# A hybrid diffusion block on one NeuronCore: scores and value products from split operands, fewer PE runs for decay and modulation, last mixer outputs kept in SBUF

## The chip, the core and the metric

The kernel runs on one core of a Trainium2 chip. The time is device time in microseconds (us) from launch to end of one execution. In this text PE is the tensor engine (matrix products), DVE the vector engine, ACT the scalar engine, POOL the GpSimd engine; SP issues most DMAs and ACT's queue issues some. SBUF is the working memory, PSUM the eight banks (128 partitions x 512 fp32) that PE writes.

## The reference, cut to what matters

Two layers over 256 latent tokens, 256 context tokens and 2,048 channels, all in fp32. Layer 0 has 16 attention heads and 32 SSD (Mamba-2) heads on one input projection; layer 1 is a gated short convolution.

```python
# layer 0: neighbourhood attention heads and bidirectional Mamba-2 heads side by side
q = rms_norm(heads(cols(p, COL_Q, ...)), q_norm_g);  k = rms_norm(...);  v = heads(...)
...
s_lat = jnp.einsum('bqhd,bkhd->bhqk', qr, kb) * scale + bias          # scores, lattice
s_ctx = jnp.einsum('bqhd,bkhd->bhqk', qr, k_ctx) * scale              # scores, context
pr = softmax(concatenate([s_lat, s_ctx]))
ya = einsum('bhqk,bkhd->bqhd', pr_lat, vb) + einsum('bhqk,bkhd->bqhd', pr_ctx, v_ctx)
...
w = cb[..., None] * decay * dtc[:, None]                              # SSD chunk of 128
y = jnp.einsum('bijgr,bjgrp->bigrp', w, xc)                           # decay product
...
out = jnp.concatenate([ya * silu(gate), yb], axis=-1) @ w_out         # 32 outputs of 128 channels
x = x + gate[:, None] * out
# every layer: shift, scale, gate = split(silu(c) @ ada_w + ada_b, 3)   (the modulation)
# layer 1: h @ w_in (4 parts), gated short convolution, @ w_out
```

The four latent rows and the 256 context tokens make 512 keys, so a head's scores are 256 queries by 512 keys, and its value product is 256 queries by 512 keys by 128 channels.

## The kernel before, in words

**Number format of the projections.** A large product a x w is made from split operands: a high half in the type fp32r (a copy of the fp32 number into that type) and a low half, the difference. Three products, high x high, low x high and high x low, go into the same bank. The weights come by DMA into `raw` buffers, ACT makes the high half `wH` (L401), DVE the low half `wL` (L408). Everything small is plain fp32 on PE: the scores (`KT` by `QT`, L1000), the value products (`Vt` by `P`, L1050), the transposes (L192), the decay products and the modulation sums. PE runs one plain fp32 product as two instructions, so the profile counts 64 for the 32 score products.

**The order is written by a planner.** Program order on each engine is made in Python at build time. The projections are the backbone: `proj` walks over K blocks and emits the backbone's products; after every few products `pump` looks at side tasks (Python generators such as `kq_gen`, `head_gen`, `group_gen`, `gemv_gen`, `mix_gen`), and lets one go on where `may` finds that the class `Plan` (a running estimate of every engine's clock and of each buffer's readiness) has its operands ready: a PE step of an attention or SSD task is placed only when they are ready 700 ns ahead of PE. Tasks hold shares of the pools: `NTMP` = 10 buffers of 128x512 (`tmp`), 9 of 128x256 (`half`), the 8 banks. `banks(n)` forces tasks on until n banks are free.

**Where the changed parts stand.** Attention runs in four groups of four heads. `kq_gen` normalises, transposes on PE, and writes K with an ACT copy into `KT` (L954) and Q with a DVE multiplication by the norm weight into `QT` (L956). `head_gen` makes two score products of 512 columns (L1000), adds the bias and takes the maximum on DVE (L1005), takes the exponential on ACT (L1010), scales on DVE (L1015), transposes on PE, copies to `PT` with ACT (L1042; two buffers, used by the heads in turn), and makes four value products of 256 columns (L1050), which DVE multiplies by the gate (L1054). `group_gen` makes, for each of 8 SSD groups, two times (b = 0, 1) four decay products of 64 output rows and 128 columns (`xtm` by `tmp`, L1358), in two separate runs; two of 64 rows stand side by side in the array. `gemv_gen` sums the modulation rows: DVE accumulates `acc` over the weights (L795), then four PE products with a matrix of ones and 32 output rows add up the partitions; there are 16 such sums. `put_mix` (L911) sends each of 32 mixer outputs (128 x 256) to DRAM, and `mix_gen` (L1478) reads them back in pairs, and ACT and DVE split them (L1488, L1489) into the buffers of the layer's input, once that input is no longer needed (`free_rows`). The output projection then reads them.

Of the kernel before, what the change touches and what calls it, by code (L numbers as in the profile page):

```python
# [31 lines left out]
for _name, _w in (("ident", 128), ("sel", 2), ("mhalf", 32), ("strip", 640), ("mask", 64)):  # L32
    _coff[_name] = (_n, _n + _w)
    _n += _w
# [107 lines left out]
def kernel(ctx: ExitStack, tc, x, cx, ada_w, ada_b, w_in, w_out, sc_in, sc_out, rpb, small, const,  # L142
# [19 lines left out]
    NTMP, NHALF, NRAW, NW = 10, 9, 5, 3  # L162
# [7 lines left out]
    KT, QT, Vt, gt = st([128, 4, 512], "KT"), st([128, 4, 256], "QT"), st([128, 4, 512], "Vt"), st([128, 4, 256], "gt")  # L170
# [68 lines left out]
    def may(task, hor, isurg):  # L239
# [17 lines left out]
        if eng == "PE":  # L257
            return rdy + (0 if isurg else 800) <= now + 100
# [71 lines left out]
    def give(pool, *bs):  # L330
        pool.extend(bs)
# [12 lines left out]
    U, ONES, L = strip[:, 128:256], strip[:, 256:384], strip[:, 384:512]  # L344
# [432 lines left out]
    acc = st([128, 512], "acc")  # L777
    n_back = [0]

    def gemv_gen():  # L780
        for n in range(16):
            lay = 0 if n < 4 else 1
            c0 = 4096 + n * 512 if n < 4 else (n - 4) * 512
            yield W_("DVE", nb=0)
            E(V.memset(acc, 0.0))
            E(DMA.dma_start(acc[:1, :], ada_b[lay:lay + 1, c0:c0 + 512]))
            for k in range(8):
                yield when(lambda: not (("gem", n, k) not in RAW))
                yield W_("DVE", RAW["gem", n, k][1], acc)
                raw, v = RAW.pop(("gem", n, k))  # L790
                ngem[0] -= 1
                for j in range(2):
                    if j:
                        yield W_("DVE", acc)
                    E(V.scalar_tensor_tensor(out=acc, in0=v[:, j], scalar=csil[:, 2 * k + j:2 * k + j + 1], in1=acc,  # L795
                                             op0=ALU.mult, op1=ALU.add))
                give_raw(raw)
                issue()
            yield W_("PE", acc, nb=1)
# [20 lines left out]
    rowb = mrb = st([128, 128], "rowb")  # L820
# [101 lines left out]
    def kq_gen(key, a, ps, nt, stat, dst, banked):  # L922
# [23 lines left out]
        for t in range(nt):  # L946
# [34 lines left out]
    b0 = rpbs[0, :, :]  # L981
    s4s = [st([128, 8], f"s4_{k}") for k in range(4)]

    def head_gen(a, h):
        hd = 4 * a + h
        bt, s4, P = bias[hd % 2], s4s[hd % 4], PT[hd % 2]
# [39 lines left out]
        yield W_("PE", KT[:, h, :], QT[:, h, :], nb=1)  # L1026
# [10 lines left out]
        scale_(1)  # L1037
        for qt in range(2):
            yield W_("PE", sps[qt], nb=1)
            pt = trans(qt)  # L1040
            yield W_("ACT", pt)
            E(S.copy(P[:, :, qt * 128:(qt + 1) * 128], four(pt)))  # L1042
# [4 lines left out]
        yield W_("PE", P, Vt, nb=1)  # L1047
# [803 lines left out]
```

## Time and profile before

| what | value |
|---|---|
| median of 3 runs (lowest to highest) | 1819.94 us (1819.16 to 1823.07) |
| profiled execution, its own time | 1820.47 us |
| its span, first to last instruction | 1818.7 us |
| granted PE clock, mean | 0.998 |
| ACT busy, share of span | 775.2 us, 43% |
| DMA moved | 376.90 MB, 207 GB/s |

A group row of the profile reads: line, engine, operation, out<-in, shapes, xcount, then busy us, mean ns of one, and the engine's idle time before them with what ended it. Matrix products are pipelined: a row's duration includes the latency, so a PE product's cost is read from the start of one to the start of the next, in the timeline. A timeline row has the start and the duration in us; equal neighbours are merged into one row.

### The profile page before, as it was taken

What the parts mean: (1) busy time and instruction counts of PE and PEld (TensorE: products, weight loads), DVE (VectorE), ACT (ScalarE), POOL (GpSimd) and SP (SyncE); (2) the same over time, 40 slices, a digit from 0 to 9 for tenths busy, and PEclk for the clock granted to TensorE, in tenths of its full rate; (3) what the DMA queues carried; (4) which work ended last, traced back from release to release, by engine and by line L of the source; (5) the groups of instructions that cost most, each with busy time, mean ns of one, the idle gap of its engine ahead of it and who ended that gap; (6) DMA issues with size and microseconds to landing.
All of it is one profiled execution on the core that took longest, in us unless ns stands there. A gap on an engine that the chain in (4) does not pass through costs nothing. (4 is left out here: it accounts for less than half of the span.)

```text
span 1818.7 us, 26323 instructions
## 1 busy us (share of the span) xinstructions
PE 1784.1 (98%) x9961; PEld 1488.1 (82%) x9961; DVE 1259.5 (69%) x2041; ACT 775.2 (43%) x1364; POOL 32.4 (2%) x28
## 2 busy tenths in 40 slices
PE   5999999999999999999999999999999999999998
PEld 4677988878888878888877898788878888888887
DVE  5566775887575877575877686776667776565665
ACT  5422543455232455232454343544445444444442
POOL 0000100001000001000001000000000000000000
PEclk9999999999999999999999999999999999999999
DMA  9987644576655576755576566678867786666664
GB/s 327 339 293 247 214 144 134 171 212 203 216 165 166 169 210 203 218 163 172 167 205 196 163 182 186 195 232 282 270 228 226 232 261 188 187 188 188 187 208 152
DMA packets 249216, 376.90 MB, mean 207 GB/s; under 512 B 32656, under 2 KB 104048, under 8 KB 249088
## 3 DMA queue, kind: packets, MB, share of 16 engines
q1 hardware_dynamic: 239792, 366.64, 65.5%
q10 hardware_dynamic: 9296, 8.57, 1.5%
q8 instruction: 78, 1.28, 0.3%
q14 instruction: 50, 0.41, 0.1%
HBM read 368.70 MB, written 7.77 MB: 207 GB/s over the span
## 5 line engine op out<-in xcount | busy, mean ns | idle before, releaser
L401 ACT CAST wH<-raw 128x1024 fp32r<-128x1024 f32 (+1 forms) x439 | 457.7, 1043 | 710.2 <-PE bank L188 556.2
L408 DVE TENSOR_TENSOR wL<-raw,wH 128x1024 fp32r<-128x1024 f32 (+1 forms) x439 | 532.0, 1214 | 283.8 <-ACT wH L401 281.3
L188 PE MATMUL bank<-h,wH 128*128 128x512 f32 x1024 | 362.4, 399 | 1.5 <-DVE h L1611 0.9
L188 PE MATMUL bank<-hH,wH 128*128 128x256 f32 (+1 forms) x1040 | 353.4, 340 | 0.8 <-ACT wH L401 0.8
L188 PE MATMUL bank<-hL,wH 128*128 128x256 f32 (+1 forms) x1040 | 337.9, 325 | 0.0
L188 PE MATMUL bank<-hH,wL 128*128 128x256 f32 (+1 forms) x1024 | 330.9, 323 | 0.9 <-DVE wL L408 0.9
L188 PE MATMUL bank<-h,wL 128*128 128x256 f32 x1024 | 287.5, 281 | 0.0
L188 PE MATMUL bank<-wH,hH 128*128 128x512 f32 x640 | 258.4, 404 | 3.9 <-ACT hH L738 2.6
L188 PE MATMUL bank<-wL,hH 128*128 128x512 f32 x640 | 251.1, 393 | 0.0
L188 PE MATMUL bank<-wH,hL 128*128 128x512 f32 x640 | 250.3, 392 | 0.1
L188 PEld LDWEIGHTS bank<-h,wH 128*128 128x128 f32 x1024 | 192.4, 188 | 50.5 <-issue 1.6
L795 DVE SCALAR_TENSOR_TENSOR acc<-raw,csil,acc 128x512 f32<-128x512 f32 x256 | 191.9, 749 | 48.5 <-DMA raw<-in_ada_w 37.9
L188 PEld LDWEIGHTS bank<-hH,wH 128*128 128x128 f32 x1040 | 196.5, 189 | 24.1 <-issue 7.2
L188 PEld LDWEIGHTS bank<-hL,wH 128*128 128x128 f32 x1040 | 196.8, 189 | 19.9 <-issue 5.0
L188 PEld LDWEIGHTS bank<-hH,wL 128*128 128x128 f32 x1024 | 193.8, 189 | 18.3 <-DVE wL L408 1.5
L188 PEld LDWEIGHTS bank<-h,wL 128*128 128x128 f32 x1024 | 193.4, 189 | 0.0
L188 PE MATMUL bank<-wH,mix 128*128 128x512 f32 x512 | 163.6, 395 | 0.0
L188 PEld LDWEIGHTS bank<-wH,hH 128*128 128x128 f32 x640 | 120.5, 188 | 35.9 <-issue 7.5
L188 PEld LDWEIGHTS bank<-wH,hL 128*128 128x128 f32 x640 | 120.5, 188 | 26.3 <-DVE hL L744 0.6
L188 PEld LDWEIGHTS bank<-wL,hH 128*128 128x128 f32 x640 | 120.8, 189 | 23.7 <-DVE wL L424 0.3
L188 PEld LDWEIGHTS bank<-wH,mix 128*128 128x128 f32 x512 | 96.1, 188 | 21.3 <-issue 1.5
L188 PE MATMUL bank<-wL,mix 128*128 128x512 f32 x256 | 99.9, 390 | 0.7 <-DVE wL L408 0.7
(246 smaller groups left out, 1665.3 us busy)
## 6 DMA issues: line engine op xcount, KB each, us to landing
raw<-in_w_in SPq DMA_DIRECT2D x208, 512.0 KB, 3.8
raw<-in_ada_w SPq DMA_DIRECT2D x165, 512.0 KB, 4.7
raw<-in_sc_in SPq DMA_DIRECT2D x128, 512.0 KB, 3.8
raw<-in_w_out SPq DMA_DIRECT2D x64, 512.0 KB, 4.8
raw<-in_sc_out SPq DMA_DIRECT2D x32, 512.0 KB, 4.8
tmp<-dram_csr SPq DMA_DIRECT2D x32, 256.0 KB, 5.5
PT<-in_ada_w SPq DMA_DIRECT2D x14, 512.0 KB, 5.8
bias<-dram_rpbs SPq DMA_DIRECT2D x64, 64.0 KB, 3.9
```

Of the source, the lines that this page charges most:

```text
L188: E(T.matmul(o, l, r, start=start, stop=stop, skip_group_check=True))
L401: E(S.copy(H, v))
L408: E(V.tensor_tensor(out=Lo, in0=v, in1=H.bitcast(F32), op=ALU.subtract))
L795: E(V.scalar_tensor_tensor(out=acc, in0=v[:, j], scalar=csil[:, 2 * k + j:2 * k + j + 1], in1=acc, op0=ALU.mult, op1=ALU.add))
```

## The change

Four things are done together.

1. **Split operands in attention.** K and Q are written as fp32r high halves, both by ACT now (`KT`, `QT`), and DVE writes the low halves `KL`, `QL` from the same bank. A score is three fp32r products in place of one fp32 product. The transposed probabilities become `PH` (ACT) and `PL` (DVE), the head's values `VH` (ACT) and `VL` (DVE), and the value product of a key block is three fp32r products in place of one. `PH` and `PL` take the memory of the two `PT` buffers, so one head's probabilities are held at a time, and a head's transposes wait until the head before has made its value products.
2. **Decay products and modulation sums in half as many runs.** A group's eight decay products are issued one behind the other into one bank (8 runs in place of 16); the modulation rows are summed two at a time, so that eight products with ones follow each other (8 runs in place of 16). A decay task holds four `tmp` buffers in place of three.
3. **Last mixer outputs in place.** Where the target buffer is already free, `put_mix` splits the output directly from its `half` buffer. In the program as built this holds for 8 of the 32 outputs; 24 still go through DRAM, with 12 reads of pairs in place of 16.
4. **Room and readiness.** `NTMP` is 9; the constant table has 256 columns fewer, and the memory kept for DMA descriptors is 1,024 bytes a partition (no GpSimd DMA is in the program). `may` counts a bank's release into the readiness of a PE step.

```diff
-    NTMP, NHALF, NRAW, NW = 10, 9, 5, 3
+    NTMP, NHALF, NRAW, NW = 9, 9, 5, 3
...
-    KT, QT, Vt, gt = st([128, 4, 512], "KT"), st([128, 4, 256], "QT"), st([128, 4, 512], "Vt"), st([128, 4, 256], "gt")
+    KT, QT, Vt, gt = st([128, 4, 512], "KT", F32R), st([128, 4, 256], "QT", F32R), st([128, 4, 512], "Vt"), st([128, 4, 256], "gt")
+    KL, QL = st([128, 4, 512], "KL", F32R), st([128, 4, 256], "QL", F32R)
...
         if eng == "PE":
+            if nb:
+                rdy = max(rdy, sorted(plan.last[b.tensor.name] for b in free_b)[nb - 1])
...
     def gemv_gen():
-        for n in range(16):
...
+        for n2 in range(0, 16, 2):
...
+            E(V.memset(accs, 0.0))
+            for n in (n2, n2 + 1):
...
+                acc = accs[:, n - n2, :]
...
+            yield W_("PE", accs, nb=1)
             ps = bank()
-            for g in range(4):
-                mm(ps[32 * g:32 * g + 32, :128], ONES[:, :32], acc[:, g * 128:(g + 1) * 128], True, True)
+            for m in range(2):
+                for g in range(4):
+                    mm(ps[32 * g:32 * g + 32, m * 128:(m + 1) * 128], ONES[:, :32], accs[:, m, g * 128:(g + 1) * 128], m == 0, True)
             yield W_("DVE", ps)
-            E(V.tensor_copy(rowb, ps[:, :128]))
+            E(V.tensor_copy(rowb, ps[:, :256]))
...
-            E(DMA2.dma_start(mrow[n // 4, (n % 4) * 512:(n % 4) * 512 + 512].rearrange("(g c) -> g c", g=4), rowb[0:128:32, :]))
+            E(DMA2.dma_start(mrow[n // 4, (n2 % 4) * 512:(n2 % 4) * 512 + 1024].rearrange("(m g c) -> g m c", m=2, g=4),
+                             two(rowb[0:128:32, :])))
...
+    mH = [None] * 32
+
     def put_mix(i, o):
+        if free_rows[0] > i % 16:
+
+            yield W_("ACT", o)
+            hl = st([128, 2, 256], f"hH{i}" if i < 16 else f"hL{i - 16}", F32R, name=f"mix{i}")
+            E(S.copy(hl[:, 0], o))
+            yield W_("DVE", hl[:, 0])
+            E(V.tensor_tensor(out=hl[:, 1], in0=o, in1=hl[:, 0].bitcast(F32), op=ALU.subtract))
+            mH[i] = hl
+            give(free_h, o)
+            return
         yield W_("AQ", o)
         E(DMA2.dma_start(mixd[i], o))
         give(free_h, o)
...
-            give(free_t, kns[t])
-            yield W_("ACT" if key == "K" else "DVE", pt)
+
+            o = slice(t * 128, (t + 1) * 128)
+            yield W_("ACT", pt)
             if key == "K":
-                E(S.copy(dst[:, :, t * 128:(t + 1) * 128], four(pt)))
+                give(free_t, kns[t])
+                E(S.copy(dst[:, :, o], four(pt)))
+                yield W_("DVE", dst[:, :, o])
+                E(V.tensor_tensor(out=low[:, :, o], in0=four(pt), in1=dst[:, :, o].bitcast(F32), op=ALU.subtract))
             else:
-                E(V.tensor_scalar(out=dst[:, :, t * 128:(t + 1) * 128], in0=four(pt), scalar1=gqk, scalar2=None, op0=ALU.mult))
+                E(S.mul(dst[:, :, o], four(pt), gqk))
+                yield W_("DVE", dst[:, :, o])
+                E(V.scalar_tensor_tensor(out=low[:, :, o], in0=four(pt), scalar=gqk, in1=dst[:, :, o].bitcast(F32),
+                                         op0=ALU.mult, op1=ALU.subtract))
+                give(free_t, kns[t])
             give(free_b, pt)
...
         def score(qt):
             ps = bank()
-            mm(ps, QT[:, h, qt * 128:(qt + 1) * 128], KT[:, h, :], True, True)
+            o = slice(qt * 128, (qt + 1) * 128)
+            mm(ps, QT[:, h, o], KT[:, h, :], True, False)
+            mm(ps, QT[:, h, o], KL[:, h, :], False, False)
+            mm(ps, QL[:, h, o], KT[:, h, :], False, True)
             return ps
...
-        yield W_("PE", KT[:, h, :], QT[:, h, :], nb=1)
+        yield W_("PE", KL[:, h, :], QL[:, h, :], nb=1)
...
+        yield when(lambda: hd < 1 or ("pv", hd - 1) in got)
+        if not PHL:
+            PHL.extend(st([128, 4, 256], f"PT{k}", F32R, name=f"P{'HL'[k]}") for k in range(2))
+        PH, PL = PHL
         for qt in range(2):
+            o = slice(qt * 128, (qt + 1) * 128)
             yield W_("PE", sps[qt], nb=1)
             pt = trans(qt)
             yield W_("ACT", pt)
-            E(S.copy(P[:, :, qt * 128:(qt + 1) * 128], four(pt)))
+            E(S.copy(PH[:, :, o], four(pt)))
+            yield W_("DVE", PH[:, :, o])
+            E(V.tensor_tensor(out=PL[:, :, o], in0=four(pt), in1=PH[:, :, o].bitcast(F32), op=ALU.subtract))
             give(free_b, pt)
         yield ("cap", 0, 0)
         yield when(lambda: ("V", a) in got and ("G", a) in got)
         yield ("grow", 0, 1)
-        yield W_("PE", P, Vt, nb=1)
+
+        yield W_("ACT", Vt)
+        VH, VL = VHL
+        vh = Vt[:, :, h * 128:(h + 1) * 128]
+        E(S.copy(VH, vh))
+        yield W_("DVE", VH)
+        E(V.tensor_tensor(out=VL, in0=vh, in1=VH.bitcast(F32), op=ALU.subtract))
+        yield W_("PE", PL, VL, nb=1)
         po = bank()
         for kt in range(4):
-            mm(po[:, :256], Vt[:, kt, h * 128:(h + 1) * 128], P[:, kt, :], kt == 0, kt == 3)
+            mm(po[:, :256], VH[:, kt], PH[:, kt, :], kt == 0, False)
+            mm(po[:, :256], VH[:, kt], PL[:, kt, :], False, False)
+            mm(po[:, :256], VL[:, kt], PH[:, kt, :], False, kt == 3)
...
-        ys, sqs = [], []
+        ys, sqs, Ds, both_rows = [], [], [], []
...
-            Ds = []
...
                 yield W_("DVE", M, Dm)
-                E(V.tensor_tensor(out=Dm, in0=Dm, in1=M, op=ALU.mult))
-                Ds.append(Dm)
-            yield W_("PE", Ds[1], nb=1)
-            py = bank()
+
+                o = rows[0][:, hh * 256:hh * 256 + 256]
+                E(V.tensor_tensor(out=o, in0=Dm, in1=M, op=ALU.mult))
+                Ds.append(o)
+            give(free_t, rows[1])
+            if b:
+                give(free_t, CB)
+            both_rows.append(rows[0])
+        yield W_("PE", Ds[3], nb=1)
+        py = bank()
+        for b in range(2):
             for c in range(2):
                 for hh in range(2):
                     c0 = (2 * gi + b) * 128 + hh * 64
-                    mm(py[64 * hh:64 * hh + 64, c * 128:(c + 1) * 128], xtm[:, c, c0:c0 + 64],
-                       Ds[hh][:, c * 128:(c + 1) * 128], c == 0, True)
-            give(free_t, *rows)
+                    mm(py[64 * hh:64 * hh + 64, b * 256 + c * 128:b * 256 + (c + 1) * 128], xtm[:, c, c0:c0 + 64],
+                       Ds[2 * b + hh][:, c * 128:(c + 1) * 128], b == 0 and c == 0, True)
+        give(free_t, *both_rows)
+        yield ("cap", 0, 4)
+        for b in range(2):
             y, sq = half(), half()
             yield W_("DVE", py)
-            E(V.tensor_tensor(out=y, in0=py[:, :256], in1=yi[:, 2 * gi + b, :], op=ALU.add))
-            give(free_b, py)
+            E(V.tensor_tensor(out=y, in0=py[:, b * 256:b * 256 + 256], in1=yi[:, 2 * gi + b, :], op=ALU.add))
+            if b:
+                give(free_b, py)
...
-        give(free_t, CB)
         ssd_done[0] += 1
-        yield ("cap", 0, 4)
...
-            spawn(side, group_gen(s, gi), 3, 4)
+            spawn(side, group_gen(s, gi), 4, 4)
...
-    mH = [None] * 32
-
     def mix_gen(ip):
-        yield when(lambda: 2 * ip in written and 2 * ip + 1 in written and free_rows[0] > (2 * ip + 1) % 16)
-        yield W_("AQ", mixd[2 * ip:2 * ip + 2])
+        pair = (2 * ip, 2 * ip + 1)
+        yield when(lambda: all(i in written or mH[i] is not None for i in pair) and free_rows[0] > (2 * ip + 1) % 16)
+        pair = [i for i in pair if mH[i] is None]
+        if not pair:
+            return
+        i0, n = pair[0], len(pair)
+        yield W_("AQ", mixd[i0:i0 + n])
         mx = tmp()
         m3 = two(mx)
-        E(DMA2.dma_start(m3, mixd[2 * ip:2 * ip + 2].rearrange("b p c -> p b c")))
+        E(DMA2.dma_start(m3[:, :n], mixd[i0:i0 + n].rearrange("b p c -> p b c")))
         yield W_("ACT", mx)
-        for j in range(2):
-            i = 2 * ip + j
+        for j, i in enumerate(pair):
             hl = st([128, 2, 256], f"hH{i}" if i < 16 else f"hL{i - 16}", F32R, name=f"mix{i}")
...
-    late = [PT[0][:, k, :] for k in range(4)] + [PT[1][:, k, :] for k in range(4)] + \
+    late = [None] * 8 + \
...
+        for k in range(2):
+            pt = st([128, 4, 256], f"PT{k}", name=f"late{k}")
+            late[4 * k:4 * k + 4] = [pt[:, q, :] for q in range(4)]
...
-        z, le, o, le.T, z, np.where(ok, 0, -1e30).astype(np.float32)], axis=1)
+        le, o, le.T, np.where(ok, 0, -1e30).astype(np.float32)], axis=1)
...
-    nc = bacc.Bacc("TRN2", target_bir_lowering=False, num_devices=1)
+    nc = bacc.Bacc("TRN2", target_bir_lowering=False, num_devices=1, dynamic_dma_scratch_size=1024)
```

**PE at the first two scores of the second attention group** (`hH`, `hL` are the halves of the layer's input, `wH`, `wL` those of the gate projection's weights). Before:

```order
L188 MATMUL bank_86<-hL_1248,wH_97 128x256
L188 MATMUL bank_86<-hH_1243,wL_100 128x256
L188 MATMUL bank_88<-KT,QT 128x512
L188 MATMUL bank_85<-KT,QT 128x512
L188 MATMUL bank_84<-hH_1243,wH_97 128x256
L188 MATMUL bank_84<-hL_1248,wH_97 128x256
```

In the change, at the same place:

```order
L189 MATMUL bank_85<-hH_1393,wL_100 128x256
L189 MATMUL bank_87<-KT,QT 128x512
L189 MATMUL bank_87<-KL,QT 128x512
L189 MATMUL bank_87<-KT,QL 128x512
L189 MATMUL bank_89<-KT,QT 128x512
L189 MATMUL bank_89<-KL,QT 128x512
L189 MATMUL bank_89<-KT,QL 128x512
L189 MATMUL bank_88<-hH_1400,wH_97 128x256
L189 MATMUL bank_88<-hL_1405,wH_97 128x256
```

Two score products have become six, still as one stretch; the backbone's products around them are the same.

**PE at the decay products of the first SSD stage** (the backbone beside them is the K projection). Before, the second of the stage's four runs:

```order
L188 MATMUL bank_89<-wH_99,hH_941 128x512
L188 MATMUL bank_89<-wL_102,hH_941 128x512
L188 MATMUL bank_89<-wH_99,hL_946 128x512
L188 MATMUL bank_90<-tmp_65,xtm 64x128
L188 MATMUL bank_90<-tmp_67,xtm 64x128
L188 MATMUL bank_90<-tmp_65,xtm 64x128
L188 MATMUL bank_90<-tmp_67,xtm 64x128
L188 MATMUL bank_88<-wH_99,hH_941 128x512
L188 MATMUL bank_88<-wL_102,hH_941 128x512
```

In the change, the first of the stage's two runs:

```order
L189 MATMUL bank_90<-wL_99,hH_1097 128x512
L189 MATMUL bank_90<-wH_96,hL_1102 128x512
L189 MATMUL bank_88<-tmp_71,xtm 64x128 x4
L189 MATMUL bank_88<-tmp_68,xtm 64x128 x4
L189 MATMUL bank_87<-wH_96,hH_1097 128x512
L189 MATMUL bank_87<-wL_99,hH_1097 128x512
```

Four runs of four products have become two runs of eight, one for each group, and the run of each group's first half (b = 0) has moved back to that of its second.

**PE from a head's transposes (`const` by `tmp`) to its value products, in the second attention group.** Before:

```order
L192 MATMUL bank_85<-const,tmp_70 128x128 x4
L192 MATMUL bank_90<-const,tmp_68 128x128 x4
L188 MATMUL bank_89<-KT,QT 128x512
L188 MATMUL bank_91<-hH_948,wH_97 128x512
L188 MATMUL bank_91<-hL_953,wH_97 128x512
L188 MATMUL bank_91<-hH_948,wL_100 128x512
L188 MATMUL bank_84<-hH_1089,wH_97 128x512
L188 MATMUL bank_84<-hL_1094,wH_97 128x512
L188 MATMUL bank_84<-hH_1089,wL_100 128x512
L188 MATMUL bank_87<-PT_110,Vt 128x256 x4
L188 MATMUL bank_91<-hH_1089,wH_97 128x512
```

In the change (the left-out rows are 13 more backbone products):

```order
L193 MATMUL bank_85<-const,tmp_66 128x128 x4
L189 MATMUL bank_84<-acc,const 32x128 x8
L193 MATMUL bank_90<-const,tmp_68 128x128 x4
L189 MATMUL bank_83<-hH_654,wH_98 128x512
L189 MATMUL bank_83<-hL_659,wH_98 128x512
L189 MATMUL bank_83<-hH_654,wL_101 128x512
...
L189 MATMUL bank_86<-hL_812,wH_98 128x512
L189 MATMUL bank_86<-hH_807,wL_101 128x512
L189 MATMUL bank_87<-PH,VH 128x256
L189 MATMUL bank_87<-PL,VH 128x256
L189 MATMUL bank_87<-PH,VL 128x256
```

Before, one score and six backbone products stood between the transposes and the value products; in the change 18 backbone products do, and the modulation sum stands beside the transposes.

More of the change, by code (lines that the diff above doesn't have):

```diff
@@ L31 @@
 _n = 0
-for _name, _w in (("ident", 128), ("sel", 2), ("mhalf", 32), ("strip", 640), ("mask", 64)):
+for _name, _w in (("ident", 128), ("sel", 2), ("mhalf", 32), ("strip", 384), ("mask", 64)):
     _coff[_name] = (_n, _n + _w)
@@ L776 @@
     M1 = st([128, 2, KB], "M1")
-    acc = st([128, 512], "acc")
+    accs = st([128, 2, 512], "acc")
     n_back = [0]
     def gemv_gen():
-        for n in range(16):
-            lay = 0 if n < 4 else 1
-            c0 = 4096 + n * 512 if n < 4 else (n - 4) * 512
+        for n2 in range(0, 16, 2):
             yield W_("DVE", nb=0)
[L785 to L791, printed above, removed]
-                for j in range(2):
[L793 to L799, printed above, removed]
+            E(V.memset(accs, 0.0))
+            for n in (n2, n2 + 1):
+                lay = 0 if n < 4 else 1
+                c0 = 4096 + n * 512 if n < 4 else (n - 4) * 512
+                acc = accs[:, n - n2, :]
+                E(DMA.dma_start(acc[:1, :], ada_b[lay:lay + 1, c0:c0 + 512]))
+                for k in range(8):
+                    yield when(lambda: not (("gem", n, k) not in RAW))
+                    yield W_("DVE", RAW["gem", n, k][1], acc)
+                    raw, v = RAW.pop(("gem", n, k))
+                    ngem[0] -= 1
+                    for j in range(2):
+                        if j:
+                            yield W_("DVE", acc)
+                        E(V.scalar_tensor_tensor(out=acc, in0=v[:, j], scalar=csil[:, 2 * k + j:2 * k + j + 1], in1=acc,
+                                                 op0=ALU.mult, op1=ALU.add))
+                    give_raw(raw)
+                    issue()
+            yield W_("PE", accs, nb=1)
@@ L818, in gemv_gen @@
                 n_back[0] = 11.5
-    rowb = mrb = st([128, 128], "rowb")
+    rowb = st([128, 256], "rowb")
+    mrb = rowb[:, :128]
     spawn(back, gemv_gen())
@@ L920, with kq_gen @@
     attn = [0]
-    def kq_gen(key, a, ps, nt, stat, dst, banked):
+    def kq_gen(key, a, ps, nt, stat, dst, low, banked):
         for t in range(nt):
@@ L981 @@
     b0 = rpbs[0, :, :]
+    PHL, VHL = [], [st([128, 4, 128], f"V{k}", F32R) for k in "HL"]
     s4s = [st([128, 8], f"s4_{k}") for k in range(4)]
@@ L1828 @@
     le, lt = one(j[:, None] <= j[None]), one(j[:, None] < j[None])
-    z, o = np.zeros((128, 128), np.float32), np.ones((128, 128), np.float32)
+    o = np.ones((128, 128), np.float32)
     const = np.concatenate([
         np.eye(128, dtype=np.float32), one((j[:, None] % 32) == np.arange(2)[None]), np.full((128, 32), -0.5, np.float32),
-        z, le, o, le.T, z, np.where(ok, 0, -1e30).astype(np.float32)], axis=1)
+        le, o, le.T, np.where(ok, 0, -1e30).astype(np.float32)], axis=1)
     strict = np.stack([lt.T, lt], axis=1)
```

13 lines of the change are left out of this document (6 added, 7 removed).

## The prediction

> **What bounds the kernel now.** I read the page first, then who waited for whom on PE, then the timeline of PE at each place that the change touches.
>
> ```profile
> PE 1784.1 (98%) x9961; PEld 1488.1 (82%) x9961; DVE 1259.5 (69%) x2041; ACT 775.2 (43%) x1364; POOL 32.4 (2%) x28
> PE   5999999999999999999999999999999999999998
> ```
>
> PE has an instruction in flight 98% of the span, and in 38 of 40 slices 90% or more. That alone could hide waiting, so the next view lists PE's waits.
>
> ```profile
> PE bank L188 <- DVE rx L582: 13.7, 1, 13.7
> PE bank L188 <- ACT hH L738: 2.6, 2, 1.4
> PE bank L188 <- ACT Vt L964: 2.4, 1, 2.4
> ```
>
> The longest, 13.7 us, is the start, which the change leaves alone. The longest in mid-run is 2.4 us. So between the first product and the last, time is what PE spends on its instructions, and a shorter PE program makes a shorter span, as long as DVE and ACT still deliver ahead of it. I price PE first, then look for new waits.
>
> **Scores.** In the timeline of PE the cost of a product is the distance between starts.
>
> ```profile
> 440.46 0.28 PE L188 MATMUL bank<-hH,wL 128*128 128x256 f32 x1
> 440.58 1.88 PE L188 MATMUL bank<-KT,QT 128*128 128x512 f32 x4
> 441.90 0.68 PE L188 MATMUL bank<-hH,wH 128*128 128x256 f32 x1
> 442.42 0.28 PE L188 MATMUL bank<-hL,wH 128*128 128x256 f32 x1
> 442.54 0.29 PE L188 MATMUL bank<-hH,wL 128*128 128x256 f32 x1
> ```
>
> A split product of 256 columns takes 0.12 us (442.42 to 442.54, or 440.46 to 440.58). Two scores (four instructions) begin at 440.58; the product behind them overlaps their end, so I count to the one after it and take its own 0.12 off: 442.42 - 440.58 - 0.12 = 1.72, or 0.86 a score.
>
> ```profile
> 305.41 0.39 PE L188 MATMUL bank<-hL,wH 128*128 128x512 f32 x1
> 305.64 0.39 PE L188 MATMUL bank<-hH,wL 128*128 128x512 f32 x1
> 305.87 1.89 PE L188 MATMUL bank<-PT,Vt 128*128 128x256 f32 x8
> 307.40 0.58 PE L188 MATMUL bank<-hH,wH 128*128 128x512 f32 x1
> 307.82 0.40 PE L188 MATMUL bank<-hL,wH 128*128 128x512 f32 x1
> ```
>
> A split product of 512 columns takes 0.23 us. Three make 0.69, against 0.86: 0.17 less, times 32 scores, is **5.4 us**. `QL` and `KL` have the shapes of `hL` and `wL`, and those run at 0.23 here in the same order of loads, so I see no reason for another price.
>
> **Value products.** In the same rows one head's four products (eight instructions) take 307.82 - 305.87 - 0.23 = 1.72. Twelve split ones of 256 columns take 12 x 0.12 = 1.44: 0.28 less, times 16 heads, is **4.5 us**.
>
> The Trainium skill ("FP8 and Floating Point Precision", section TensorE Precision Notes) says that true FP32 takes four passes through the array. By it three passes for four would save a quarter: 0.23 a score and 0.48 a head, 7.4 + 7.7 in place of 5.4 + 4.5, and the time would be some 5 us lower. The rows decide otherwise: plain fp32 costs 0.86 us where four split products would cost 0.92, so I keep the smaller saving.
>
> **Decay products and modulation sums.** The number of products stays; the runs halve.
>
> ```profile
> 390.34 0.66 PE L188 MATMUL bank<-tmp,xtm 128*64 128x128 f32 x8
> 390.92 0.50 PE L188 MATMUL bank<-wH,hH 128*128 128x512 f32 x1
> 391.26 0.40 PE L188 MATMUL bank<-wL,hH 128*128 128x512 f32 x1
> ...
> 393.22 0.43 PE L188 MATMUL bank<-acc,const 128*32 128x128 f32 x8
> 393.58 0.50 PE L188 MATMUL bank<-wH,hH 128*128 128x512 f32 x1
> 393.92 0.40 PE L188 MATMUL bank<-wL,hH 128*128 128x512 f32 x1
> ```
>
> A decay run costs 391.26 - 390.34 - 0.23 = 0.69; a modulation run 393.92 - 393.22 - 0.23 = 0.47. What would a second half cost, if it follows directly? The trace has no such doubled run. From below it could be free, and each joining would save the whole run (0.69 or 0.47); from above it costs all of it again and nothing is saved. For a middle value I use the plain fp32 rate at 128 columns:
>
> ```profile
> 437.56 1.04 PE L192 MATMUL bank<-const,tmp 128*128 128x128 f32 x8
> 438.36 0.36 PE L188 MATMUL bank<-hH,wH 128*128 128x256 f32 x1
> 438.56 0.28 PE L188 MATMUL bank<-hL,wH 128*128 128x256 f32 x1
> ```
>
> Eight such instructions take 438.56 - 437.56 - 0.12 = 0.88, so 0.11 each. Decay instructions go two side by side (64 of 128 output rows each), so eight need 4 x 0.11 = 0.44 and the run has 0.25 of entry and exit; modulation sums go four side by side, 2 x 0.11 = 0.22, again with 0.25 left over. I take that 0.25 as saved once for each run that disappears: 8 + 8 runs, **4.0 us**, between 0 and 8 x 0.69 + 8 x 0.47 = 9.3.
>
> **What DVE and ACT get in return.** Counts: 16 `KL` and 32 `PL` subtractions of 512 columns from PSUM, 16 `VL` from SBUF, 8 `QL` in place of 8 `QT`; on ACT 8 `QT` and 16 `VH`.
>
> ```profile
> L1523 DVE TENSOR_TENSOR tmp<-bank,tmp 128x512 f32<-128x512 f32 x8 | 5.5, 685 | 1.5 <-PE bank L188 1.5
> L1526 DVE TENSOR_TENSOR x1a<-tmp,tmp 128x512 f32<-128x512 f32 x4 | 2.8, 692 | 0.1
> L1042 ACT COPY PT<-bank 128x512 f32<-128x512 f32 x32 | 17.9, 589 | 35.6 <-PE bank L192 34.3 <-DMA dram_csr<-tmp 1.3
> ```
>
> DVE: 48 x 0.685 + 16 x 0.692 = 44.0 us more (69% to 72% of the span). ACT: 24 x 0.589 = 14.1 more, less the issue of 12 DMAs for mixer outputs and 8 for the modulation. Both have room on average; what counts is each stretch. Four heads bring 8 `PL` and 4 `VL` to the place of their value products, 8.2 us.
>
> ```profile
> 440.00:520.00 80.00, 80.00 (x385) 63.79 (x384) 49.25 (x85) 25.76 (x41) 0.00 (x0) 1.00 0.64 194
> 1140.00:1180.00 40.00, 36.90 (x175) 29.70 (x174) 28.90 (x65) 23.63 (x55) 1.14 (x1) 1.00 0.67 200
> 1180.00:1220.00 40.00, 40.00 (x188) 31.84 (x187) 29.36 (x56) 18.16 (x29) 0.70 (x1) 1.00 0.73 220
> ```
>
> (Columns: stretch, length, then busy PE, PEld, DVE, ACT, POOL, clock, DMA share, GB/s.) In the second group's stretch DVE goes from 49.3 to 57.5 of 80 us: covered. The last stretch is tighter: 58.3 of 80 us before, 8.2 more from the heads, and the SSD tasks that now come later there.
>
> **New waits.** A value product now waits for ACT's `PH`, then DVE's `PL`, then `VL` (behind ACT's `VH`, which runs beside `PL`): 0.589 + 0.685 + 0.692 = 2.0 us at least after the last transpose. The order shows 18 backbone products there, 18 x 0.23 = 4.1 us, so 2.1 us are left for whatever stands ahead on DVE. Behind a waiting `PL` on DVE stand the next head's work and the weights' low halves, which PE needs next; three `wL` buffers lie between. If this cover were gone, each head would cost up to 2.0 us. The wait of a head's transposes for the head before costs PE nothing while the backbone has products to put there; what it holds are two `tmp` buffers. Nine of them, with four for a decay task, move the SSD groups later, where the order lets the backbone run on. Should a bank be missing at the start of a projection, PE would stop: I put that, with all other new waits, at 1 us net, between -3.1 (the 40 - 36.9 us that PE idles in 1140 to 1180 disappear, since eight outputs skip DRAM there) and +8.2 (all DVE work of the last four heads shows).
>
> **Sum.** 5.4 + 4.5 + 4.0 - 1.0 = 12.9 us. The profiled execution took 1820.5 (1.8 more than its span), half a us above the median of 1819.9; from the median the sum gives **1807 us**.
>
> **Rivals.**
> - *DVE binds in the last stretch.* For it: 58.3 + 8.2 of 80 us plus later SSD work, and PE's largest mid-run wait is there. Against: the order puts those outputs dozens of backbone products before their use. All 8.2 us in place of my 1.0 gives 1814.
> - *More is gained.* The last stretch loses its 3.1 us of idle PE, and joined runs save more than 0.25: 1807 - 4.1 - 2 gives about 1801.
> - *The heads' chain is exposed.* If DVE's queue ahead of each `PL` holds over 2.1 us (two weight low halves of 1.2 us would do), the 18 products no longer cover the chain. At 2.0 us for each of 16 heads that is 32 us, and the time is about 1838. It becomes slower than before from 0.9 us a head. Against it: in 440 to 520 DVE has 30 us free of 80, and PE waits nowhere there.
> - *The change does less than it says.* Of the mixer outputs only 8 of 32 stay in SBUF, which I priced at nothing apart from the bound above. If joined runs save nothing, 1811.
>
> The Trainium skill ("TensorE: Matmul & The Clock Gate", What's actually happening) states that after an idle window of about 3.4 us the PE clock falls to half. That would make the third rival worse; the longest mid-run wait, 2.4 us, left the clock at 1.00 here, and no row shows a longer one there.
>
> **Chances.** My forecast, 1803 to 1811: 0.62. DVE in the last stretch, 1811 to 1817: 0.18. More gained, under 1803: 0.08. No net change, 1817 to 1823: 0.06. Exposed chain, over 1823: 0.06. The range to hold 8 of 10 takes in the DVE rival and the near part of the greater gain: 1801 to 1816. A measurement of this kernel can tell about 0.2% (3.6 us) from no change: faster than 1816.3 has 0.85, within 0.2% 0.09, slower 0.06.
>
> **What would show it.** Right: `KT,QT`, `KL,QT` and `KT,QL` starting 0.23 us apart; a head's twelve value products in 1.44 us; decay runs of 16 instructions in 1.13 us and modulation runs in 0.69; PE idle outside the start still about 7 us; DVE near 1304 us busy. Wrong: waits of PE on `PL` or `VL` (exposed chain), on `wL` between 1140 and 1220 us (DVE bound), or on a bank at the start of a projection (pools too small).

## The result, and the profile after

The changed kernel takes 1802.1 us (median of 4 runs, 1800.2 to 1804.0) against 1820.0 (4 runs, 1819.2 to 1823.1): 17.9 us less, a ratio of 0.990 (95% interval 0.9886 to 0.9915). The forecast was 1807, with 1801 to 1816 as its range: the right sign, cheaper PE work as the cause, and 5 us too little.

First the page of the changed kernel, PE's busy time and its forty slices:

```profile
PE 1766.6 (98%) x10057; PEld 1493.8 (83%) x10057; DVE 1295.0 (72%) x2089; ACT 788.1 (44%) x1388; POOL 32.8 (2%) x28
PE   5999999999999999999999999999999999999998
```

PE is still the bound at 98%. It has 96 instructions more and is busy 17.5 us less: the products became cheaper, not fewer. DVE and ACT took on 35.5 and 12.9 us of busy time, and the end does not show it.

The waits of PE, in the order of the view (total, times, longest):

```profile
PE bank L189 <- DMA raw<-in_ada_w: 14.3, 2, 14.0
PE bank L189 <- ACT hH L741: 2.6, 2, 1.4
PE bank L189 <- ACT Vt L993: 1.3, 1, 1.3
PE bank L189 <- DVE wL L411: 1.2, 3, 0.6
```

The start is as before. The wait in the last stretch (the row that names `Vt`) went from 2.4 to 1.3 us. All 15 rows of this view without the start add up to 12.0 us; before they were also 15 rows, with 15.0. So there are 3.0 us of waiting less, where I had allowed for 1.0 more. No row names `PL`, `VL` or a `tmp` for more than 0.2 us.

PE's timeline at the changed places (start, duration, instruction):

```profile
278.44 0.39 PE L189 MATMUL bank<-hH,wL 128*128 128x512 f32 x1
278.68 0.28 PE L189 MATMUL bank<-PH,VH 128*128 128x256 f32 x1
278.79 0.28 PE L189 MATMUL bank<-PL,VH 128*128 128x256 f32 x1
...
279.96 0.28 PE L189 MATMUL bank<-PH,VL 128*128 128x256 f32 x1
280.08 0.40 PE L189 MATMUL bank<-hH,wH 128*128 128x512 f32 x1
...
440.83 0.40 PE L189 MATMUL bank<-KT,QT 128*128 128x512 f32 x1
441.06 0.40 PE L189 MATMUL bank<-KL,QT 128*128 128x512 f32 x1
441.30 0.39 PE L189 MATMUL bank<-KT,QL 128*128 128x512 f32 x1
...
442.22 0.28 PE L189 MATMUL bank<-hH,wH 128*128 128x256 f32 x1
...
657.25 0.65 PE L189 MATMUL bank<-acc,const 128*32 128x128 f32 x16
657.82 0.51 PE L189 MATMUL bank<-wH,hH 128*128 128x512 f32 x1
658.16 0.39 PE L189 MATMUL bank<-wL,hH 128*128 128x512 f32 x1
...
675.75 1.09 PE L189 MATMUL bank<-tmp,xtm 128*64 128x128 f32 x16
676.77 0.50 PE L189 MATMUL bank<-wH,hH 128*128 128x512 f32 x1
677.11 0.40 PE L189 MATMUL bank<-wL,hH 128*128 128x512 f32 x1
```

- A head's value products: 280.08 - 278.68 = 1.40 us (1.72 before): 0.32 x 16 = 5.1 us.
- Two scores: 442.22 - 440.83 = 1.39 us (1.72 before): 0.165 x 32 = 5.3 us.
- A joined modulation run: 658.16 - 657.25 - 0.23 = 0.68 us, where two runs took 0.94: 0.26 x 8 = 2.1 us.
- A joined decay run: 677.11 - 675.75 - 0.23 = 1.13 us, where two took 1.38: 0.25 x 8 = 2.0 us.

That is 14.5 us of price and 3.0 us of waits, 17.5 together. The medians lie 17.9 us apart, but the rows come from two profiled executions that lie 20.3 apart (1820.5 and 1800.2; the one is 0.4 above its median, the other 1.9 below). So in the profiles 2.8 us are not explained: PE's busy time alone fell by 17.5, and the four rows price 14.5 of it. That the sum comes so near to the medians is in part luck.

DVE in the stretches that the prediction watched (stretch, length, then busy PE, PEld, DVE, ACT, POOL, clock, DMA share, GB/s):

```profile
440.00:520.00 80.00, 80.00 (x399) 66.73 (x398) 55.44 (x97) 27.54 (x45) 0.00 (x0) 1.00 0.63 194
1140.00:1180.00 40.00, 38.05 (x204) 31.28 (x201) 32.72 (x72) 27.08 (x57) 0.81 (x1) 1.00 0.63 186
1180.00:1220.00 40.00, 40.00 (x207) 33.45 (x206) 29.08 (x56) 21.57 (x36) 0.70 (x1) 1.00 0.62 192
...
580.00:596.00 16.00, 16.00 (x136) 15.96 (x135) 15.49 (x20) 10.41 (x13) 0.00 (x0) 1.00 0.58 178
```

In the second group's stretch DVE has 55.4 of 80 us (57.5 forecast), in the last 61.8 of 80. PE idles 2.0 us in these two rows, 3.1 before. The last row is a stretch that I had not looked at: DVE is busy 15.5 of 16 us there, and PE does not wait for it.

### The profile page after: what moved, and what is told of

It reads as the page before. It is cut to its first block, busy times and chain, and to the rows that moved or that the text cites. A ratio compares the mean times of both kernels' runs of the same rounds, so it can differ in the third digit from the quotient of the medians.

```text
span 1798.3 us, 26561 instructions
## 1 busy us (share of the span) xinstructions
PE 1766.6 (98%) x10057; PEld 1493.8 (83%) x10057; DVE 1295.0 (72%) x2089; ACT 788.1 (44%) x1388; POOL 32.8 (2%) x28
## 5 line engine op out<-in xcount | busy, mean ns | idle before, releaser
L189 PE MATMUL bank<-hH,wH 128*128 128x256 f32 (+1 forms) x1040 | 343.3, 330 | 0.9 <-ACT wH L404 0.9
```

The source lines that it names most:

```text
L189: E(T.matmul(o, l, r, start=start, stop=stop, skip_group_check=True))
```

## The experiments

The kernels ran in four groups, each group beside runs of the kernel before; ratios are to those. The medians of the kernel before were 1821.3, 1819.5, 1819.1 and 1819.8 us. Its single runs lay between 1812.7 and 1823.5, so 1 or 2 us between two kernels decide nothing. Where a time is set against "the changed kernel", that is the 1801.8 us of the second group, if nothing else is said.

| kernel | median us | ratio to before (95%) | PE's waits without the start, us |
|---|---|---|---|
| changed kernel, again | 1801.8 | 0.9903 (0.9889 to 0.9917) | 12.9 |
| plain value products | 1802.4 | 0.9907 (0.9893 to 0.9922) | 11.1 |
| plain scores | 1816.6 | 0.9980 (0.9970 to 0.9990) | 19.3 |
| cut runs | 1802.2 | 0.9902 (0.9881 to 0.9923) | 12.6 |
| cut runs, again | 1805.5 | 0.9923 (0.9907 to 0.9939) | 12.9 |
| mixer outputs through DRAM | 1800.9 | 0.9894 (0.9880 to 0.9909) | 12.4 |
| score price, order fixed | 1808.2 | 0.9942 (0.9929 to 0.9954) | 13.6 |
| value price, order fixed | 1806.7 | 0.9929 (0.9916 to 0.9941) | 12.1 |
| `PL` three times | 1812.4 | 0.9958 (0.9943 to 0.9973) | 20.0 |
| without the rule for banks | 1809.2 | 0.9942 (0.9924 to 0.9960) | 18.3 |
| before + joined runs | 1812.3 | 0.9962 (0.9947 to 0.9977) | 11.7 |
| before + the rule for banks | 1820.9 | 1.0008 (0.9997 to 1.0019) | 12.6 |

The last column is the sum over the rows of PE's waits in each kernel's one profile.

### The changed kernel once more

> The changed kernel again, beside the runs of this group: 1802 us, and 0.990 of the kernel before.

1801.8 us and 0.9903. Its profile has 12.9 us of waits, the first had 12.0: a difference below 1 us in this sum is not one between kernels. This profiled execution (1801.5) lies 18.9 us below the one of the kernel before, and here the sum closes better: 14.5 of price, 2.1 of waits, and 1.7 of clock, since a stretch of half clock near 28 us, which the other two profiles have, is missing (it is shown in the last section). That is 18.3 of 18.9.

### Plain value products

```diff
-            E(S.copy(PH[:, :, o], four(pt)))
-            yield W_("DVE", PH[:, :, o])
-            E(V.tensor_tensor(out=PL[:, :, o], in0=four(pt), in1=PH[:, :, o].bitcast(F32), op=ALU.subtract))
+            E(S.copy(P[:, :, o], four(pt)))
...
-            mm(po[:, :256], VH[:, kt], PH[:, kt, :], kt == 0, False)
-            mm(po[:, :256], VH[:, kt], PL[:, kt, :], False, False)
-            mm(po[:, :256], VL[:, kt], PH[:, kt, :], False, kt == 3)
+            mm(po[:, :256], Vt[:, kt, h * 128:(h + 1) * 128], P[:, kt, :], kt == 0, kt == 3)
```

> The changed kernel, with the value products as before (four plain fp32 products a head, two P tiles by turns, no low halves of P and V). Theory 1 (the price of the products decides): in the changed trace twelve split products of a head that stand alone take 1.40 us against 1.73 for the four plain ones, so 16 x 0.33 = 5.2 us come back: 1807.3 us from 1802.1. Theory 2 (the new chain of P and V costs waits or DVE time that eat part of the price): less than 3.5 us come back. DVE's busy time falls by 32 x 0.69 + 16 x 0.69 = 33 us by both.

Two `P` tiles are used by turns, and `VH`, `VL` go too. 1802.4 us: the median speaks for theory 2. But the profiled run (1804.6 us, the second slowest of five) shows PE from its first product to its last 1784.5 us long (1797.6 - 13.0), against 1779.1 (1793.1 - 14.0) in the changed kernel: the 5.4 us of the price are in it. DVE falls by 27.6 us (1295.0 to 1267.4), not by 33. Since the planner makes another order from other products, this kernel does not measure the price alone.

### Plain scores

```diff
-            mm(ps, QT[:, h, o], KT[:, h, :], True, False)
-            mm(ps, QT[:, h, o], KL[:, h, :], False, False)
-            mm(ps, QL[:, h, o], KT[:, h, :], False, True)
+            mm(ps, QT[:, h, o], KT[:, h, :], True, True)
...
-    KL, QL = st([128, 4, 512], "KL", F32R), st([128, 4, 256], "QL", F32R)
```

> The changed kernel, with each score as one plain fp32 product, and without the low halves of K and Q. Theory 1: a pair of split products for a score takes 0.69 us where one plain product took 0.86, so 32 x 0.17 = 5.5 us come back: 1807.6 us. Theory 2 (the price is right but the added subtractions hold PE): under 4 us come back.

`QT` is written by DVE again. 1816.6 us, 14.8 more than the changed kernel: both theories missed it. Its waits of PE show two that the changed kernel does not have:

```profile
PE bank L189 <- DVE wL L411: 3.3, 3, 2.7
PE bank L189 <- DVE half L1423: 3.1, 1, 3.1
```

and its timeline shows that the second of them costs more than 3.1 us:

```profile
957.90 0.40 PE L189 MATMUL bank<-hH,wL 128*128 128x512 f32 x1
961.40 0.98 PE L189 MATMUL bank<-const,half 128*128 128x1 f32 x4 [3.10 <-DVE half L1423]
...
965.23 0.63 PE L189 MATMUL bank<-hH,wL 128*128 128x512 f32 x1
965.66 0.63 PE L189 MATMUL bank<-hH,wH 128*128 128x512 f32 x1
...
968.49 0.40 PE L189 MATMUL bank<-hL,wH 128*128 128x512 f32 x1
968.73 0.39 PE L189 MATMUL bank<-hH,wL 128*128 128x512 f32 x1
```

Behind the wait, products that elsewhere start 0.23 us apart start 0.43 apart (965.23 to 965.66), until about 968.2. The windows give the granted clock (the column behind POOL):

```profile
960.00:965.00 5.00, 3.60 (x22) 3.16 (x23) 4.89 (x11) 4.94 (x32) 0.13 (x1) 0.65 0.73 204
965.00:969.00 4.00, 4.00 (x13) 3.10 (x12) 2.59 (x7) 0.55 (x5) 0.57 (x1) 0.59 0.88 275
```

0.65 and 0.59, and 1.00 from 969 on: 5 x 0.35 + 4 x 0.41 = 3.4 us of clock are lost on top of 3.1 us of waiting. Behind the longest wait for `wL` (2.7 us, up to 1165.95) the clock drops too:

```profile
1166.20:1169.70 3.50, 3.50 (x9) 2.69 (x9) 3.50 (x7) 1.58 (x3) 0.00 (x0) 0.51 0.64 174
```

That is 3.5 x 0.49 = 1.7 us more, 5.1 in all; the first profile of the changed kernel has one such loss of 1.7 us (last section). The two profiled executions lie 16.1 us apart (1816.3 and 1800.2), and three parts make them up: 5.3 for the price of the scores, 19.3 - 12.0 = 7.3 for waits of this kernel's own order, and 5.1 - 1.7 = 3.4 for the clock behind waits, 16.0 together.

### Price of scores and of value products, order fixed

```diff
+    def mm_as(o, l, r, start, stop, ns):
+        plan.over = ns
+        mm(o, l.bitcast(F32), r.bitcast(F32), start, stop)
+        plan.over = None
...
-            mm(ps, QT[:, h, o], KT[:, h, :], True, False)
-            mm(ps, QT[:, h, o], KL[:, h, :], False, False)
-            mm(ps, QL[:, h, o], KT[:, h, :], False, True)
+            mm_as(ps, QT[:, h, o], KT[:, h, :], True, True, 3 * (9 + 0.434 * 512))
```

The planner is told the time of three split products, so every engine keeps the order of the changed kernel. The second kernel does the same to `VH` and `PH`, with 256 columns.

> The changed kernel in its own order on every engine, only that each score is one plain fp32 product of the high halves (the low halves are still computed and not used: the score is that of rounded K and Q). Theory 1 (plain scores cost their price alone, and the other 9 us that the kernel with plain scores lost came from two waits of about 3 us that its other order brought, and from the lower clock behind them): +5.5 us against the changed kernel, PE's idle time within 1 us of its 12.5, clock 0.998 or more. Theory 2 (plain products themselves lower the clock or hold PE): +12 us or more.

> The changed kernel in its own order on every engine, only that a head's value products are four plain fp32 ones of the high halves (the low halves are still computed and not used: the products are those of rounded P and V). Theory 1 (the price of the products): +5.2 us against the changed kernel, as the spans of PE in the profiles of the two earlier kernels have it (+5.4). Theory 2 (the medians of the earlier group are right and the value products' split brought next to nothing): within 1.5 us of the changed kernel.

1808.2 and 1806.7 us: 6.4 and 4.9 us above the changed kernel beside them, where 5.5 and 5.2 were expected. Waits differ by less than 1 us. Theory 1 holds in both: with the order held, these two splits are worth their price, and the other 8 us of the kernel with plain scores came with its order. The low halves are still made in both kernels, so what that work on DVE costs by itself is not in these numbers.

### Cut runs, twice

```diff
         for b in range(2):
+            if b:
+                at_ = n_mm[0]
+                yield when(lambda: n_mm[0] > at_)
             for c in range(2):
```

The same stands in the loop of the modulation sums; `n_mm` counts products.

> The changed kernel, with each joined run of decay products and of modulation sums cut in two: the second half goes out only when another product stands between. All other work is the same. Theory 1 (0.25 us of entry and exit for each run): 16 more runs cost 4.0 us, 1806.1 us, and a half run takes 0.70 us (decay) or 0.46 (modulation) in the timeline where the whole takes 1.13 or 0.69. Theory 2 (what the joining brought came from the order around it, not from the runs): within 1 us of 1802.1.

> The kernel with cut runs a second time, since its first six runs lay between 1797 and 1810 us. Theory 1 (the price of 16 more runs, 4.0 us, is there, and the first median was low by chance): 1805 to 1807 us. Theory 2 (its other order gains about as much as the cuts cost): 1802 again, with PE's idle time or its time at a lower clock below that of the changed kernel in the profile.

1802.2 and 1805.5 us, with single runs from 1797.2 to 1809.6. In both profiles a half decay run costs 0.70 us and a half modulation run 0.46 (medians of 13 that stand between other products), so the cuts do cost 16 x 0.25 us in PE's timeline. The time shows between 0 and 4 us of it. The two groups do not agree, and the waits do not explain the first: this stays open. One thing that can make such a kernel scatter stands in the first profile: one wait of 1.4 us near 1148, and the clock behind it.

```profile
1147.00:1150.00 3.00, 1.57 (x8) 1.26 (x8) 2.74 (x8) 2.38 (x6) 0.00 (x0) 0.87 0.36 105
1150.00:1153.00 3.00, 3.00 (x10) 2.36 (x9) 2.36 (x6) 3.00 (x9) 0.00 (x0) 0.56 0.72 251
```

### Joined runs alone, on the kernel before

The parts of the diff that concern `accs`, `rowb`, `Ds`, `both_rows`, the cap of a group's tasks and the smaller `strip`; ten `tmp` buffers fit.

> The kernel before with one part of the change alone: decay products and modulation sums in joined runs (scores, value products, mixer outputs, the rule for banks and the ten tmp buffers as before). Theory 1 (each run that disappears saves 0.25 us): 16 runs fewer, 4.0 us less, a ratio of 0.9978. Theory 2 (the order around them decides, as the median of the kernel with cut runs suggests): within 1 us of the kernel before, or another value that PE's idle time explains.

1812.3 us: 6.9 less than the kernel before in its group, more than the price of 4.0. Its waits are 11.7 us where the kernel before has 15.0. In the kernel before, the longest of them stood ahead of a decay run of the last stretch:

```profile
1162.42 1.07 ACT L1488 CAST mix<-tmp 128x256 fp32r<-128x256 f32 x3 [1.02 <-DMA tmp<-dram_mixd]
1164.66 1.55 ACT L964 COPY Vt<-bank 128x512 f32<-128x512 f32 x3
1165.28 0.73 PE L188 MATMUL bank<-tmp,xtm 128*64 128x128 f32 x8 [2.42 <-ACT Vt L964]
```

What ended it, as far as the view can tell, was ACT's copy of a bank into `Vt`; ahead of that copy ACT had stood 1.02 us for a mixer output from DRAM. The kernel with joined runs has no row for `Vt`; the new ones are short:

```profile
PE bank L188 <- DVE half L1387: 0.9, 1, 0.9
...
PE bank L188 <- DVE mix L1502: 0.8, 1, 0.8
```

So 4.0 of price and 3.3 of waits, 7.3 together. The joined run goes out later than its first half used to, and PE no longer stands before it. How much of the 3.3 us the joining brings is less sure than the price: each kernel has one profile, and the kernel before with the rule for banks (below) has 12.6 us of waits in its profile without a lower median.

### Mixer outputs through DRAM

```diff
-        if free_rows[0] > i % 16:
+        if False:
```

> The changed kernel, with all 32 mixer outputs through DRAM as before. Theory 1 (the eight outputs in place removed the wait of the last stretch): PE's idle time between 1130 and 1170 us goes from 1.95 us back to 3 or more, and the time rises by 1 to 2 us, to 1803 to 1804. Theory 2 (the wait became shorter because the SSD groups' work moved): the same time within 0.7 us, idle time as in the changed kernel.

1800.9 us, and the waits are 12.4: no loss, and no sign of the wait of the last stretch coming back. Between 1130 and 1170 us PE idles 1.2 us, and the row for `Vt` is 0.5 us (1.3 in the changed kernel). Theory 2. The eight outputs in place bring nothing that can be measured.

### The rule for banks

```diff
-            if nb:
-                rdy = max(rdy, sorted(plan.last[b.tensor.name] for b in free_b)[nb - 1])
```

> The changed kernel without its two lines in the rule that lets a task go to PE (a bank's last reader is then not looked at for urgent tasks). Theory 1 (these lines removed waits of PE for a bank): PE's idle time rises from 12.5 to 14 us or more, the time to 1803.5 or more. Theory 2 (they do not matter): within 1 us of the changed kernel's 1802, idle time 12 to 13.5.

> The kernel before with the two lines of the rule for PE alone. Theory 1 (the rule only makes up for waits that the other parts of the change bring to the order): within 1.5 us of the kernel before, PE's idle time 14.5 to 16.5 us. Theory 2 (the rule removes waits by itself, the 3 us of idle time that the changed kernel lacks): 3 us less or more, a ratio of 0.9985 or below, with idle time near 12.5.

Without the rule the changed kernel takes 1809.2 us, 7.4 more than the changed kernel's 1801.8. Its waits:

```profile
PE bank L189 <- DVE wL L409: 3.8, 4, 2.0
...
PE bank L189 <- DVE tmp L1399: 2.1, 1, 2.1
...
PE bank L193 <- DVE KL L977: 1.5, 2, 0.9
```

`KL` in the last row is the new subtraction that reads a bank before PE may write it again: the transposes stood on PE ahead of it. Given to the kernel before, the rule alone changes nothing (1.0008, though the one profile of it, its fastest run, has 12.6 us of waits). So the rule alone does not bring the gain, but without it the changed kernel loses 7 us of it. The waits are 6.3 us more (18.3 against 12.0), and only 1.5 of them name one of the added readers of banks; that these readers are why the rule is needed is argued, not shown.

### `PL` three times

```diff
             E(V.tensor_tensor(out=PL[:, :, o], in0=four(pt), in1=PH[:, :, o].bitcast(F32), op=ALU.subtract))
+            for _ in range(2):
+                V.tensor_tensor(out=PL[:, :, o], in0=four(pt), in1=PH[:, :, o].bitcast(F32), op=ALU.subtract)
```

> The changed kernel in its own order, with each low half of P computed three times (64 subtractions of 0.685 us more, 44 us of DVE; the output is the same). In the changed trace the value products start 0.06 to 3.35 us after the last subtraction of their chain. Theory 1 (the chain is covered, thinly, by the products between): a chain that is 1.37 us longer is late for five heads of sixteen, 1.31 + 0.92 + 0.21 + 0.15 + 0.03 = 2.6 us in all, so the time rises by 2 to 5 us. Theory 2 (DVE has no room in these stretches): 10 us or more, with PE waiting for weights' low halves.

1812.4 us, 10.6 more: by its size this is theory 2, and its waits are of both kinds.

```profile
PE bank L189 <- DVE wL L411: 4.2, 5, 2.4
...
PE bank L189 <- DVE tmp L1403: 1.9, 3, 0.7
...
PE bank L189 <- DVE PL L1084: 1.6, 3, 0.7
...
PE bank L189 <- DVE VL L1095: 0.9, 4, 0.2
```

`PL` and `VL` together are 2.5 us, where the slack of each head (the time from the end of its chain to its first value product) had given 2.6. The sum agrees in part by chance: four heads wait, near 288, 304, 507 and 782 us, and the head whose slack was least, 0.06 us, is not one of them. The rest of the 8 us of new waits is mostly DVE's queue behind the longer chain, above all one wait of 2.4 us for a weight's low half at 597 us, about where DVE was full in the changed kernel already, and the clock behind it:

```profile
590.00:594.00 4.00, 4.00 (x37) 4.00 (x36) 3.90 (x6) 1.05 (x1) 0.00 (x0) 1.00 0.62 190
594.00:597.00 3.00, 0.61 (x6) 0.40 (x4) 2.96 (x5) 2.23 (x3) 0.00 (x0) 0.99 0.26 96
597.00:600.00 3.00, 3.00 (x14) 3.00 (x15) 2.96 (x5) 0.63 (x1) 0.00 (x0) 0.50 0.59 174
```

44 us of DVE spread over the whole run cost a quarter of their length.

## Why the prediction was right, and where it was short

- **The range and the chances.** The range held, 1801 to 1816, but only by its lower end: 1802.1 lies outside the forecast's own 1803 to 1811 and under the mark of the greater gain (under 1803), to which I had given 0.08. Of the 4.9 us between 1807 and 1802.1, 4.0 are the term for waits and 0.6 the value products.
- **PE's price bounds the time.** Right. The two splits with the order fixed cost 6.4 and 4.9 us when undone; the joined runs alone bring 6.9, of which 4.0 are price by the rows.
- **Scores, 5.4 us.** Right: 5.3 in the timeline, 6.4 in the time.
- **Value products, 4.5 us.** Too small: 5.1 in the timeline, 4.9 in the time. I used 0.12 us for a product of 256 columns; twelve in a row take 1.40 us, 0.117 each, and 192 of them make the rounding into 0.6 us.
- **Merged runs, 4.0 us.** The middle value was right: joined runs take 1.13 and 0.68 us, so 0.25 is saved once for each run that disappears. That the rivals' ends (0 or 9.3 us) were out is read from these rows. In the time of the changed kernel the cut runs showed 0 to 4 us, and this is open.
- **New waits, 1.0 us more.** This is the step that failed: there are 2 to 3 us less. I saw the bound (-3.1, PE's idle time in the last stretch) and took a value near nothing. The total came near the bound, but not from the place that I had named: the idle time there went from 3.1 to 2.0 us, and the rest is spread over other rows. I also gave the bound a wrong cause: I put it down to the mixer outputs that skip DRAM, and without them in place the waits are the same. The joined decay run on the kernel before removes 3.3 us of waits, among them the one that stood before a decay run. That it does the same inside the changed kernel is likely, not shown. The rival of a greater gain (1801) had the size of this term about right and the runs wrong.
- **PE idle outside the start, "still about 7 us".** This sign was misread before the change: the rows of PE's waits add up to 15.0 us there, and to 12.0 after.
- **The rule on four passes.** My estimate from the four passes of the Trainium skill ("FP8 and Floating Point Precision", TensorE Precision Notes), a quarter saved, was 7.4 + 7.7 us; the runs show 5.3 + 5.1. The rows were the better price, though the total by that estimate (18.1 with the other terms) came out nearer to the whole gain, for another reason: the waits. The 0.23 and 0.48 are quarters of four split products; quarters of the measured 0.86 and 1.72 us would be 6.9 + 6.9.
- **The rival of the exposed chain.** Its cover held: in both profiles of the changed kernel all sixteen heads have their `VL` before PE is ready for it. It is thin, though: the least is 0.06 us in one profile and 0.94 in the other, and with 1.37 us more of chain PE waits three times for `PL` and four times for `VL`. A chance of 0.06 was fair for this order, but my reason (DVE's room over 80 us) did not see how thin it is; what stands on DVE ahead of one subtraction seems to decide.
- **DVE busy 1304 us.** 1295.0; the new groups came as forecast, and where the 9 us went was not followed.

## What to carry to other kernels

When PE is the bound, price a change from the distance between starts in its own timeline, part by part; here the two splits, undone one at a time with the order held, cost 6.4 and 4.9 us for 5.3 and 5.1 in the timeline. The joined runs were not measured so: their 4.0 us are read from rows, and undoing them cost 0 to 4. Undoing a part in a kernel whose order a planner makes measures the new order too: 14.8 us for a price of 5.3. A wait of one to three us on PE can cost 1.7 us more than its length through the clock (3.4 in one case here), and a change that adds readers of a PSUM bank should tell the planner of them.

## What the runs showed of the hardware

PE's granted clock drops to half behind some waits in mid-run, for about 3.5 us, in one case for 7. It did so behind 3.10 us (0.65, then 0.59), 2.4 us (0.50) and 1.4 us (0.87, then 0.56), and it did not behind 2.42 us in the kernel before, whose windows are these:

```profile
1163.00:1166.00 3.00, 0.72 (x9) 0.55 (x9) 1.63 (x5) 3.00 (x7) 0.00 (x0) 1.00 0.45 140
1166.00:1169.00 3.00, 2.32 (x10) 1.63 (x10) 2.46 (x5) 3.00 (x8) 0.00 (x0) 1.00 0.26 87
```

So the length of one wait does not decide it. The two profiles of the changed kernel say more: the same program, with the same wait at the same place, has the drop in the first and not in the second.

```profile
27.21 0.74 PE L189 MATMUL bank<-wH,hH 128*128 128x512 f32 x2 [1.22 <-ACT hH L741]
28.60:32.10 3.50, 3.50 (x10) 2.75 (x9) 3.45 (x5) 3.39 (x8) 0.00 (x0) 0.51 1.04 383
...
27.31 0.73 PE L189 MATMUL bank<-wH,hH 128*128 128x512 f32 x2 [1.22 <-ACT hH L741]
28.60:32.10 3.50, 3.50 (x15) 2.46 (x15) 3.40 (x6) 3.11 (x7) 0.00 (x0) 1.00 1.02 359
```

The first loses 3.5 x 0.49 = 1.7 us by it. The kernel before has such a drop too, 0.50 from 27.8 to 31.2 us behind 1.22 us of waiting; the prediction looked only behind the longest wait in mid-run and missed it.

The Trainium skill ("TensorE: Matmul & The Clock Gate", What's actually happening) gives an idle window of about 3.4 us. The length of one drop here, about 3.5 us, is near that, but none of these waits lasted 3.4 us: the drops stand behind waits of 1.22 to 3.10 us. What else counts (what PE did just ahead of the wait, or where a window begins) was not tried.
